# The first feed-forward's out product in two column blocks, four of 22 row pairs of each by seven products

## The chip, the cores and the metric

The kernel runs on one core of one Trainium2 chip. A core has a matrix engine (TensorE, PE in the profile; its weight loads are PEld), a vector engine (VectorE, DVE), a scalar engine (ScalarE, ACT), GpSimd (POOL) and SyncE (SP), which here issues most DMAs. Each engine runs its own instructions in order; semaphores tie them together. Operands lie in SBUF, sums of products in PSUM. The metric is the device time of one execution in microseconds (us), the median of several runs; lower is better.

## The reference

The layer takes x (256 positions of 2048 channels) and 256 memory positions:

```python
x += 1/2 * SwiGLU_1(rms(x))        # h = silu(gate) * up, 5632 wide; then h @ w_out
h = rms(x); p = h @ w_mix_in       # conv value | conv gate | gMLP u | gMLP v
x += concat(rms(conv(p)), rms(gmlp(p))) @ w_mix_out
x += CrossAttn_4heads(rms(x), rms(mem))
x += 1/2 * SwiGLU_2(rms(x))
out = rms_norm(x)
```

All in float32. The change concerns `h @ w_out` of the first SwiGLU, a product of 256 x 5632 by 5632 x 2048, and what stands right behind it: the first products of `w_mix_in`.

## The kernel before

**Products.** Each operand is kept as two parts, a rounded high part and the rest (low part), and a product of float32 matrices is three products of parts: high by high, high by low, low by high. ScalarE makes the high part by a cast, VectorE the low part by a subtraction (`weights`, lines 115 and 116, for weights; `split`, lines 123 and 124, for the other operand). A weight tile is 128 rows (one k) by 1024 columns or two k by 512, 512 KB, loaded by SyncE's queue into one of the "raw" tiles and split into an "hl" tile. TensorE uses it in twelve products of 128x128 by 128x512: two halves of the 256 positions, two halves of the columns (or two k), three products of parts.

**First feed-forward, in product.** The class `FeedForward` makes eleven column groups h0 to h10 of the hidden layer. Each h tile has 512 columns, that is four k of the out product. Within a group the 16 k go in eight pairs, some of them "S": a pair by `seven`, the others "C": by `eight`. A pair of k and a pair of column halves of 512 with the two halves of positions is a 2x2 by 2x2 block product, eight products; `seven` (Winograd's form of Strassen's scheme) makes it with seven, from sums of weight blocks (made on VectorE, lines 422 to 435) and from four sums of blocks of the other operand, "forms" or sides, that are made once. Its seven results gather in seven accumulators, "1" to "7", which are joined at the end with those of `eight` ("2", "3", "4", "8").

**Turns.** The out product needs h with its columns on the partitions. `turning` (line 293) makes four 128x128 transposes on TensorE into one PSUM tile "aux"; of these there are two. `split` then writes the result into hA, hB or hC: a cast on ScalarE, a subtraction on VectorE. A turn covers two k, so there are 22. Four are done in the last group of the in product.

**Out product.** `gemm_n` goes over four blocks of 512 columns, each over the 44 k two at a time (22 weight tiles): lines 190 to 192. In the first block one of the remaining 18 turns is issued after each weight tile (`between=turns`). Each block's result is copied by ScalarE into a tile o, turned in two turns, and joined to xT (`joins`, line 637) in the course of the next product:

```python
for n in range(4):
    acc = gemm_n(a["ffn1_w_out"][n], ff.of, per=0.8 if n else 0.0, between=turns, after=0 if n == 0 else 4)
    ...
    turns += [turning(o, 2 * i * P, joins(4 * n + 2 * i)) for i in range(2)]
```

Then the mix stage starts: `gemm_n` over the column groups of `w_mix_vg`, four products that also carry the last turns. `later`, `put` and `beside` hold a list of small jobs (squares of the memory rows, convolution taps) that are dealt out behind weight tiles by a cost in us.

**What sets the order.** The program is written as straight code for a tile framework; pools hand out buffers (wraw 4 weight tiles, whl 3 split tiles, ps 6 and pa 2 PSUM banks), and a scheduler lays out each engine's instructions from it.

Of the kernel before, what the change touches and what calls it, by code (L numbers as in the profile page):

```python
# [11 lines left out]
F32 = mybir.dt.float32  # L12
# [5 lines left out]
P = 128  # L18
# [20 lines left out]
SUMMED = ((2, 7, 13), (2, 7, 13))  # L39

# [29 lines left out]
def layer(ctx: ExitStack, tc: tile.TileContext, a: dict):  # L70
# [108 lines left out]
    def gemm_n(w, x_hl, per=0.0, between=None, after=4):  # L179

        acc = [ps.tile([P, 2, 256], F32, name="acc").rearrange("p a b -> p (a b)") for _ in range(2)]
        nk = w.shape[1]
        for k0 in range(0, nk, 2):
# [9 lines left out]
            if between and k0 >= after:  # L193
                between.pop(0)()
            beside(per)
        return acc
# [132 lines left out]
    class FeedForward:  # L329
# [6 lines left out]
        def __init__(self, stack, tags, x_hl, gain, w_in, pattern, summed):  # L336
# [41 lines left out]
        def raw(self, j, k):  # L378
            i = self.raw_at % (4 + len(self.raws))
            self.raw_at += 1  # L380
            raw = wraw.tile([P, 1024], F32, name="raw") if i < 4 else self.raws[i - 4]
            nc.sync.dma_start(out=raw, in_=self.w_in[j, :, k])
            return raw
# [28 lines left out]
        def x(self, k, t):  # L412
            s = slice(t * P, (t + 1) * P)
            return self.x_hl[:, k, 0, s], self.x_hl[:, k, 1, s]

        def seven(self, j, p, b, first, last):
# [8 lines left out]
            form = [(self.forms[self.spairs.index(p)][:, f, 0], self.forms[self.spairs.index(p)][:, f, 1]) for f in range(4)]  # L425
            three(b["5"], form[0], w[:, 0, lo], w[:, 1, lo], first, last)
            three(b["7"], form[2], w[:, 0, hi], w[:, 1, hi], first, last)
            nc.vector.tensor_tensor(out=one[:, lo], in0=sums[:, lo], in1=two[:, hi], op=ALU.add)
            w = self.parts(one)
            three(b["6"], form[1], w[:, 0, lo], w[:, 1, lo], first, last)  # L430
            three(b["1"], self.x(k, 0), w[:, 0, hi], w[:, 1, hi], first, last)
            w = self.parts(two)
            three(b["2"], self.x(k + 1, 0), w[:, 0, lo], w[:, 1, lo], first, False)
            three(b["3"], form[3], w[:, 0, hi], w[:, 1, hi], first, False)
            nc.vector.tensor_tensor(out=two[:, lo], in0=two[:, lo], in1=one[:, lo], op=ALU.subtract)
            w = self.parts(two, G)
            three(b["4"], self.x(k + 1, 1), w[:, 0, lo], w[:, 1, lo], first, False)
            if self.next is not None:
                with tc.issue_after(self.cast.ins):
                    self.summed(self.next)  # L440
                self.next = None

        def eight(self, j, p, b, first, last, plain):
            for k in (2 * p, 2 * p + 1):
                at = (j, k) in self.sums_at and self.sums_at.index((j, k))
                w = self.parts(self.raw(j, k), last=plain) if at is False else self.hls[at % len(self.hls)]
                begin = [(1, 1)] if first and k % 2 == 0 else []
                acc = [[b["2"], b["3"]], [b["4"], b["8"]]]
                by_two(acc, self.x_hl[:, k], w[:, 0], w[:, 1], k, begin, last and k % 2 == 1)
# [13 lines left out]

        def group(self, j, r, after=()):
            b = {}
            for name in "57":
                b[name] = bank(ps if name == "5" else pa, "acc" if name == "5" else "aux")
            b["6"] = bank(pa, "aux")
            for name in "1234":
                b[name] = bank(ps, "acc")  # L470
            b["8"] = bank(ps, "acc")
# [3 lines left out]
            for p, c in enumerate(self.pattern):  # L475
                if c == "S":
                    self.seven(j, p, b, p == 0, p == self.spairs[-1])
                    if p == self.spairs[-1]:
                        nc.scalar.copy(out=p1, in_=b["1"])
                        nc.vector.tensor_tensor(out=u2, in0=p1, in1=b["6"], op=ALU.add)  # L480
                        nc.vector.tensor_tensor(out=u4, in0=u2, in1=b["5"], op=ALU.add)
                        nc.vector.tensor_tensor(out=u2, in0=u2, in1=b["7"], op=ALU.add)
                        nc.vector.tensor_tensor(out=u5, in0=u2, in1=b["5"], op=ALU.add)
                else:
                    late = p > self.spairs[-1] and len(after) > 0
                    self.eight(j, p, b, p == self.pattern.index("C"), p == n - 1, late)
# [6 lines left out]
            self.give(j, (p1, u2), (u4, u5), r)  # L493

# [57 lines left out]
        def turn(self, i):  # L552

            def go():
# [10 lines left out]
                def both(tp):  # L565
                    tile, at = self.where(2 * i)
                    d = tile[:, at:at + 2]
                    split(d[:, :, 0], d[:, :, 1], tp)

# [14 lines left out]
    with ExitStack() as stack:  # L584
        ff = FeedForward(stack, ("S1", "S0", "S2"), x_hl, lambda k: gains[:, k:k + 1], a["ffn1_w_in"], PATTERNS[0], SUMMED[0])
# [45 lines left out]
        x_hl = gained_tile("S2")  # L631
        ss = st.tile([P, T], F32, name="ss", bufs=2)

        def joins(f):

            def go(tp):
# [3 lines left out]
                for k in range(f, f + 2):  # L640
                    gained(x_hl, k, xT[:, k], col("mix_norm", k))
# [3 lines left out]
        for n in range(4):  # L645
            acc = gemm_n(a["ffn1_w_out"][n], ff.of, per=0.8 if n else 0.0, between=turns, after=0 if n == 0 else 4)
            if n == 0:
                pool = stack.enter_context(ff.late)
                pool = stack.enter_context(tc.tile_pool(name="ffn1", bufs=1, reuse_waits="tile"))
            o = pool.tile([P, 2, G], F32, name="o", bufs=2)  # L650
            for t in range(2):
                nc.scalar.copy(out=o[:, t], in_=acc[t])
            turns += [turning(o, 2 * i * P, joins(4 * n + 2 * i)) for i in range(2)]
        ff.high.close()
# [4 lines left out]
    with ExitStack() as stack:  # L659
        with tc.tile_pool(name="mix", bufs=1) as pool:  # L660
# [70 lines left out]
            for n in range(NCT // 2):  # L731
                load_gate(n)
                later.appendleft((1.6, memory_parts(n)))
                acc = gemm_n(a["w_mix_vg"][n], lambda k: x_hl[:, k], per=1.35, between=turns, after=2)
# [423 lines left out]
def _laid_out(v):  # L1158
# [17 lines left out]
    a["ffn1_w_out"] = _tiled(g["ffn1_w_out"][0], 512)  # L1176
# [31 lines left out]
```

## Time and profile before

| | |
|---|---|
| median of 3 runs | 2100.37 us (2097.94 to 2103.01) |
| profiled execution, own time | 2096.62 us |
| its span | 2094.9 us |
| TensorE busy | 2082.5 us (99%) |
| VectorE busy | 1577.4 us (75%) |
| ScalarE busy | 1165.2 us (56%) |
| GpSimd busy | 67.7 us (3%) |
| moved by DMA | 442.34 MB |

The span runs from the first to the last instruction; the own time of the same execution is 1.7 us longer. Busy time of an engine that others wait for sets the time; busy time of the others matters only where they are late. The out product of the first feed-forward runs from 467 to 716 us of the span.

### The profile page before, as it was taken

Reading aid. Unit: us, or ns where it says so; the run is one execution under the profiler, and the core shown is the slowest. Engines: PE = TensorE matmul, PEld = TensorE weight load, DVE = VectorE, ACT = ScalarE, POOL = GpSimd, SP = SyncE. Lnnn points to the kernel's source line nnn. Section 1 sums busy time; section 2 is a strip of 40 time slices with the busy share of each in tenths; the row PEclk is TensorE's granted clock in tenths of the full one; section 3 lists DMA queues with packets and bytes.
Section 4 is the critical chain, followed back from the end, with each engine's and each line's share of the span. In section 5 each row is a group of like instructions: output and inputs, shape, how many; then the busy total and the mean of one; then the engine's idle time right before and its main releaser. Section 6 shows DMA issues by size and latency. Waiting matters only on the chain.

```text
span 2094.9 us, 26646 instructions
## 1 busy us (share of the span) xinstructions
PE 2082.5 (99%) x9786; PEld 1741.6 (83%) x9786; DVE 1577.4 (75%) x2217; ACT 1165.2 (56%) x1451; POOL 67.7 (3%) x83
## 2 busy tenths in 40 slices
PE   9999999999999999999999999999999999999998
PEld 7888888888888888888888898888888888888886
DVE  7888888875655589888877666778888888787754
ACT  8665666554544454445665454556665666554443
POOL 0000000000000000000000000000000000000000
PEclk9999999999999999999999999999999999999999
DMA  9787778755665666555555543576777777556664
GB/s 368 241 263 246 226 228 263 228 183 169 226 189 188 216 233 198 187 180 183 182 197 188 186 157 117 200 272 218 217 248 251 241 225 246 182 163 203 195 192 152
DMA packets 122387, 442.34 MB, mean 211 GB/s; under 512 B 13584, under 2 KB 13968, under 8 KB 121872
## 3 DMA queue, kind: packets, MB, share of 16 engines
q1 hardware_dynamic: 113040, 407.08, 57.0%
q0 software_dynamic: 8640, 32.51, 8.3%
q8 instruction: 76, 1.25, 0.2%
q10 hardware_dynamic: 576, 1.06, 0.1%
q14 instruction: 55, 0.45, 0.1%
HBM read 438.49 MB, written 2.10 MB: 210 GB/s over the span
## 4 chain that ended last, share of the span: by engine, by line
PE 96%; DMA 2%; issue 1%; ACT 1%; DVE 0%; POOL 0%; SPq 0%; DVEq 0%; ACTq 0%; POOLq 0%
PE acc L192 12%; PE acc L191 12%; PE acc L190 12%; PE acc L319 9%; PE acc L321 9%; PE acc L318 9%; PE acc L144 8%; PE acc L151 4%; PE acc L307 3%; PE acc L305 3%; PE acc L306 3%; PE aux L293 1%; PE aux L307 1%; PE aux L305 1%; PE aux L306 1%
## 5 line engine op out<-in xcount | busy, mean ns | idle before, releaser
L116 DVE TENSOR_TENSOR hl<-raw,hl 128x1024 fp32r<-128x1024 f32 (+1 forms) x402 | 488.5, 1216 | 277.3 <-ACT hl L115 276.3
L115 ACT CAST hl<-raw 128x1024 fp32r<-128x1024 f32 (+1 forms) x402 | 419.6, 1045 | 477.8 <-PE acc L192 291.0
L373 DVE TENSOR_TENSOR hl<-spare,hl 128x1024 fp32r<-128x1024 f32 (+1 forms) x128 | 146.6, 1149 | 34.0 <-ACT hl L372 31.0
L372 ACT CAST hl<-spare 128x1024 fp32r<-128x1024 f32 (+1 forms) x128 | 126.2, 994 | 69.4 <-PE acc L321 25.9
L319 PE MATMUL acc<-hl,x_hl 128*128 128x512 f32 x408 | 147.7, 391 | 0.3 <-DVE hl L124 0.2
L373 DVE TENSOR_TENSOR hl<-raw,hl 128x1024 fp32r<-128x1024 f32 (+1 forms) x107 | 120.7, 1131 | 29.7 <-ACT hl L372 28.3
L372 ACT CAST hl<-raw 128x1024 fp32r<-128x1024 f32 (+1 forms) x107 | 103.5, 979 | 69.6 <-PE acc L321 26.7
L318 PE MATMUL acc<-hl,x_hl 128*128 128x512 f32 x408 | 141.8, 390 | 0.3 <-ACT hl L123 0.3
L321 PE MATMUL acc<-hl,x_hl 128*128 128x512 f32 x408 | 126.5, 389 | 0.0
L372 ACT CAST ring<-spare 128x1024 fp32r<-128x1024 f32 (+1 forms) x81 | 80.4, 997 | 58.9 <-PE acc L321 19.0
L373 DVE TENSOR_TENSOR ring<-spare,ring 128x1024 fp32r<-128x1024 f32 (+1 forms) x81 | 93.0, 1153 | 13.9 <-ACT ring L372 12.6
L191 PE MATMUL acc<-hl,m_hl 128*128 128x512 f32 x256 | 100.3, 392 | 0.0
L191 PE MATMUL acc<-hl,x_hl 128*128 128x512 f32 x256 | 100.3, 392 | 0.0
L192 PE MATMUL acc<-hl,m_hl 128*128 128x512 f32 x256 | 100.2, 391 | 0.0
L192 PE MATMUL acc<-hl,x_hl 128*128 128x512 f32 x256 | 99.8, 390 | 0.0
L319 PE MATMUL acc<-ring,x_hl 128*128 128x512 f32 x248 | 91.4, 389 | 0.0
L190 PE MATMUL acc<-hl,m_hl 128*128 128x512 f32 x256 | 91.2, 392 | 0.0
L318 PEld LDWEIGHTS acc<-hl,x_hl 128*128 128x128 f32 x408 | 76.4, 188 | 16.6 <-ACT hl L123 0.5
L319 PEld LDWEIGHTS acc<-hl,x_hl 128*128 128x128 f32 x408 | 76.2, 188 | 16.8 <-DVE hl L373 0.8
L190 PE MATMUL acc<-hl,x_hl 128*128 128x512 f32 x256 | 90.0, 391 | 0.0
L321 PEld LDWEIGHTS acc<-hl,x_hl 128*128 128x128 f32 x408 | 76.6, 188 | 16.0
L318 PE MATMUL acc<-ring,x_hl 128*128 128x512 f32 x248 | 88.8, 389 | 0.0
(362 smaller groups left out, 4974.9 us busy)
## 6 DMA issues: line engine op xcount, KB each, us to landing
spare<-in_ffn_w_in SPq DMA_DIRECT2D x195, 512.0 KB, 7.0
raw<-in_ffn_w_out SPq DMA_DIRECT2D x176, 512.0 KB, 3.5
raw<-in_ffn_w_in SPq DMA_DIRECT2D x156, 512.0 KB, 6.4
hl_s<-in_ffn_w_in POOLq DMA_DIRECT2D x44, 512.0 KB, 8.8
raw<-in_w_mix_vg SPq DMA_DIRECT2D x32, 512.0 KB, 4.5
raw<-in_w_k SPq DMA_DIRECT2D x32, 512.0 KB, 3.6
raw<-in_w_v SPq DMA_DIRECT2D x32, 512.0 KB, 4.3
raw<-in_w_mix_out SPq DMA_DIRECT2D x32, 512.0 KB, 4.6
```

What stands on the lines that cost most here:

```text
L115: nc.scalar.copy(out=hl[:, 0, :size], in_=raw[:, :size])
L116: newest[0] = nc.vector.tensor_tensor(out=hl[:, 1, :size], in0=raw[:, :size], in1=hl[:, 0, :size].bitcast(F32), op=ALU.subtract)
L144: nc.tensor.matmul(acc, lhsT=hi[:, k], rhs=xs[k], start=first and k == 0, stop=last and k == kk - 1, skip_group_check=True,)
L151: nc.tensor.matmul(acc[:, 0], lhsT=lo[:, k], rhs=xs[k][:, 0], start=False, stop=last and k == kk - 1, skip_group_check=True,)
L190: nc.tensor.matmul(acc[t], lhsT=x[:, 0, s], rhs=hi[:, k], start=k0 + k == 0, stop=False)
L191: nc.tensor.matmul(acc[t], lhsT=x[:, 0, s], rhs=lo[:, k], start=False, stop=False)
L192: nc.tensor.matmul(acc[t], lhsT=x[:, 1, s], rhs=hi[:, k], start=False, stop=k0 + k == nk - 1)
L318: nc.tensor.matmul(acc[t][g], lhsT=x[:, 0, s], rhs=hi[:, cols[g]], start=(t, g) in first, stop=False)
L319: nc.tensor.matmul(acc[t][g], lhsT=x[:, 0, s], rhs=lo[:, cols[g]], start=False, stop=False)
L321: nc.tensor.matmul(acc[t][g], lhsT=x[:, 1, s], rhs=hi[:, cols[g]], start=False, stop=last)
L372: self.cast = nc.scalar.copy(out=hl[:, 0, :n], in_=raw[:, :n])
L373: newest[0] = nc.vector.tensor_tensor(out=hl[:, 1, :n], in0=raw[:, :n], in1=hl[:, 0, :n].bitcast(F32), op=ALU.subtract)
```

## The change

The out product is made in two blocks of 1024 columns. Each block goes over 22 pairs of k; pairs 9, 12, 15 and 18 are made by `seven`, the others by `eight`, with the eight accumulators of the in product ("6" and "7" in the two aux banks). The first block takes the pairs in order; the second starts with pair 9 and has the three others behind every second plain pair. The weights are laid out anew in memory for it. The sides of the four pairs are made when their k are turned (`out_sides`): a copy on ScalarE, four operations of 128x128 on VectorE, and two splits of 256 elements each. The remaining 18 turns are issued within the first seven pairs: three in each of the first four, two in each of the next three; behind pair 6 a pool is opened over memory of h4 to h10, for the sums of weights, two more raw tiles (raw_out) and the result. Three tiles of "more_out" take the place of x_hl meanwhile: two for split weights, the rest for the sides. The second block's result is joined in four turns during the first products of the mix stage; the first two of these are made in halves, first k 0 to 7 of both, then k 8 to 15.

In numbers of instructions: 24 products of 128x512 fewer on TensorE, 88 instructions more on VectorE, 22 more on ScalarE, the same number of DMAs. The orders of all engines are unchanged up to the start of the out product, and from the product by w_mix_out on.

```diff
+OUT_S = (9, 12, 15, 18)
+OUT_STEPS = (
+    list(range(KF // 2)),
+    [9, 0, 1, 12, 2, 3, 15, 4, 5, 18, 6, 7, 8, 10, 11, 13, 14, 16, 17, 19, 20, 21],
+)
...
-        def eight(self, j, p, b, first, last, plain):
+        def eight(self, j, p, b, last, plain, between=None):
             for k in (2 * p, 2 * p + 1):
+                if between is not None and k % 2 == 1:
+                    between()
...
+        def out_block(self, n, result, hook, between=None):
+            b = {}
+            self.begun = set()
+            steps = OUT_STEPS[n]
+            for i, p in enumerate(steps):
+                if p in OUT_S:
+                    if "5" not in b:
+                        self.banks(b, "57612348" if i == 0 else "5761")
+                    done = all(q not in OUT_S for q in steps[i + 1:])
+                    self.seven(NG + n, p, b, done)
+                    if done:
+                        o = result()
+                        places = [o[:, t, g * G:(g + 1) * G] for g in range(2) for t in range(2)]
+                        self.joins_sevens(b, *places)
+                else:
+                    if i == 0:
+                        self.banks(b, "2348")
+                    self.eight(NG + n, p, b, i == len(steps) - 1, False, between)
+                hook(i)
+            for acc, i in (("2", 0), ("3", 2), ("4", 1), ("8", 3)):
+                nc.vector.tensor_tensor(out=places[i], in0=places[i], in1=b[acc], op=ALU.add)
+            return o
+
+        def out_sides(self, form, tp):
+            f1, f2 = ev.tile([P, T], F32, name="tu"), ev.tile([P, T], F32, name="tg")
+            second = ev.tile([P, T], F32, name="sq")
+            nc.scalar.copy(out=second.rearrange("p (k t) -> p k t", k=2), in_=tp[:, :, P:])
+            a11, a21, a12, a22 = tp[:, 0, :P], second[:, :P], tp[:, 1, :P], second[:, P:]
+            f = [f1[:, :P], f1[:, P:], f2[:, :P], f2[:, P:]]
+            nc.vector.scalar_tensor_tensor(out=f[0], in0=a21, scalar=-1.0, in1=a22, op0=ALU.mult, op1=ALU.subtract)
+            nc.vector.scalar_tensor_tensor(out=f[1], in0=f[0], scalar=-1.0, in1=a11, op0=ALU.mult, op1=ALU.subtract)
+            nc.vector.tensor_tensor(out=f[2], in0=a11, in1=a21, op=ALU.subtract)
+            nc.vector.tensor_tensor(out=f[3], in0=a12, in1=f[1], op=ALU.subtract)
+            for i, both in enumerate((f1, f2)):
+                s = slice(2 * i, 2 * i + 2)
+                split(form[:, s, 0], form[:, s, 1], both.rearrange("p (f n) -> p f n", f=2))
...
-        for n in range(4):
-            acc = gemm_n(a["ffn1_w_out"][n], ff.of, per=0.8 if n else 0.0, between=turns, after=0 if n == 0 else 4)
...
+        def turns_first(i):
...
+            for _ in range(2 if i < 4 else 1):
+                next_turn()
+            if i == 6:
+                stack.enter_context(ff.late)
+                ff.high.close()
+                pool = rest["pool"] = stack.enter_context(tc.tile_pool(name="ffn1", bufs=1, reuse_waits="tile"))
+                ff.sums = pool.tile([P, 1024], F32, name="sums_out")
+                ff.raws += [pool.tile([P, 1024], F32, name=f"raw_out{q}") for q in range(2)]
...
+        o = ff.out_block(0, result, turns_first, next_turn)
+        turns += turned(o, 0)
...
+        o = ff.out_block(1, result, beside_second)
+        turns += turned(o, 1)
...
+            accs = []
+            for n in range(2):
+                load_gate(n)
+                later.appendleft((1.6, memory_parts(n)))
+                accs.append(gemm_n(
+                    a["w_mix_vg"][n], lambda k: x_hl[:, k], per=1.35, between=turns, after=0, ks=range(0, 8, 2), step=4
+                ))
```

**Turns in TensorE's order.** Before, in the first block of the out product, around the turns of h8 and h9 (h_128 and h_129 are their tiles, ident the identity matrix, hB the turned operand of this block's k):

```order
L192 MATMUL acc<-hl,hB 128x512
L190 MATMUL acc<-hl,hB 128x512 x2
L191 MATMUL acc<-hl,hB 128x512 x2
L293 MATMUL aux<-ident,h_128 128x128 x4
L293 MATMUL aux<-ident,h_129 128x128 x4
L192 MATMUL acc<-hl,hB 128x512 x2
L190 MATMUL acc<-hl,hB 128x512
L191 MATMUL acc<-hl,hB 128x512
L192 MATMUL acc<-hl,hB 128x512
```

Two turns stand together, and weight tiles of products ahead of and behind them. With the change, at the same point of the turns (first rows: the last products of k 13, last two rows: the first products of k 14):

```order
L329 MATMUL acc<-hl,hA 128x512 x2
L326 MATMUL acc<-hl,hA 128x512
L301 MATMUL aux<-ident,h_127 128x128 x4
L327 MATMUL acc<-hl,hA 128x512
L326 MATMUL acc<-hl,hA 128x512
L327 MATMUL acc<-hl,hA 128x512
L329 MATMUL acc<-hl,hA 128x512 x2
L301 MATMUL aux<-ident,h_128 128x128 x8
L301 MATMUL aux<-ident,h_129 128x128 x8
L301 MATMUL aux<-ident,h_130 128x128 x8
L326 MATMUL acc<-hl,hA 128x512 x4
L327 MATMUL acc<-hl,hA 128x512 x2
```

The six turns of h8, h9 and h10 have moved together, between the products of two weight tiles.

**Casts in ScalarE's order.** Before, for the turns of h7 to h10 (hB and hC from aux are the turns' casts, hl from raw those of weight tiles):

```order
L123 CAST hB<-aux 128x2x256 x2
L115 CAST hl<-raw 128x1024 x2
L123 CAST hB<-aux 128x2x256
L123 CAST hC<-aux 128x2x256
L115 CAST hl<-raw 128x1024 x2
L123 CAST hC<-aux 128x2x256 x2
L115 CAST hl<-raw 128x1024
L241 ACTIVATE sm<-raw 128x256
L244 ACTIVATE sq<-raw 128x256 x2
L115 CAST hl<-raw 128x1024
```

At most two casts of turns stand together there. With the change, from the copy for the sides of h7's second turn to the cast of the weight tile of k 14 (raw_out):

```order
L552 COPY sq<-aux 128x256
L131 CAST hB<-aux 128x2x256
L131 CAST more_out<-tu 128x2x128
L131 CAST more_out<-tg 128x2x128
L131 CAST hB<-aux 128x2x256
L131 CAST hC<-aux 128x2x256
L552 COPY sq<-aux 128x256
L131 CAST hC<-aux 128x2x256
L131 CAST more_out<-tu 128x2x128
L131 CAST more_out<-tg 128x2x128
L131 CAST hC<-aux 128x2x256 x2
L381 CAST hl<-raw_out_3907 128x1024
```

The cast of the weight tile has moved behind the casts of all six turns and of their sides (tu and tg).

**VectorE's order, with the change,** from the sides of h7's second turn to those of h9's first (before, VectorE had no such operations; the turns' subtractions stood between those of weight tiles):

```order
L555 SCALAR_TENSOR_TENSOR tu<-sq 128x128
L556 SCALAR_TENSOR_TENSOR tu<-tu,aux 128x128
L557 TENSOR_TENSOR tg<-aux,sq 128x128
L132 TENSOR_TENSOR hB<-aux,hB 128x2x256
L558 TENSOR_TENSOR tg<-aux,tu 128x128
L132 TENSOR_TENSOR more_out<-tu,more_out 128x2x128
L132 TENSOR_TENSOR more_out<-tg,more_out 128x2x128
L132 TENSOR_TENSOR hB<-aux,hB 128x2x256
L132 TENSOR_TENSOR hC<-aux,hC 128x2x256
L555 SCALAR_TENSOR_TENSOR tu<-sq 128x128
L556 SCALAR_TENSOR_TENSOR tu<-tu,aux 128x128
L557 TENSOR_TENSOR tg<-aux,sq 128x128
```

The last operation on the sides (line 558, which reads aux) has moved behind the subtraction of the turn that follows.

## Rows read from the trace of the kernel before

**Rows 1.** Page: span, and TensorE's busy time, share and instructions.

```profile
span 2094.9 us, 26646 instructions
...
PE 2082.5 (99%) x9786; PEld 1741.6 (83%) x9786; DVE 1577.4 (75%) x2217; ACT 1165.2 (56%) x1451; POOL 67.7 (3%) x83
```

**Rows 2.** Windows of the out product: us, PE, PEld, DVE, ACT, POOL busy, clock.

```profile
467.00:527.00 60.00, 60.00 (x301) 50.20 (x300) 37.18 (x43) 31.65 (x42) 0.00 (x0) 1.00 0.53 167
...
653.00:716.00 63.00, 63.00 (x285) 52.18 (x284) 33.08 (x40) 30.56 (x39) 0.00 (x0) 1.00 0.57 182
```

**Rows 3.** Waits of TensorE, the longest of six.

```profile
PE aux L219 <- DVE ones L216: 1.1, 1, 1.1
```

**Rows 4.** Timeline of TensorE in the out product's second block, weight tiles' starts.

```profile
563.40 0.62 PE L190 MATMUL acc<-hl,hB 128*128 128x512 f32 x2
...
579.72 0.62 PE L190 MATMUL acc<-hl,hB 128*128 128x512 f32 x2
```

**Rows 5.** Timeline of TensorE in the last group, a tile with a turn.

```profile
458.00 1.07 PE L318 MATMUL acc<-hl,x_hl 128*128 128x512 f32 x4
458.91 0.60 PE L293 MATMUL aux<-ident,h 128*128 128x128 f32 x4
...
461.20 0.62 PE L318 MATMUL acc<-hl,x_hl 128*128 128x512 f32 x2
```

**Rows 6.** Timeline of three engines, two turns in the out product.

```profile
508.50 1.03 PE L293 MATMUL aux<-ident,h 128*128 128x128 f32 x8
...
509.14 1.07 ACT L123 CAST hB<-aux 128x512 fp32r<-128x512 f32 x2 [0.29 <-PE aux L293]
...
510.02 1.28 DVE L124 TENSOR_TENSOR hB<-aux,hB 128x512 fp32r<-128x512 f32 x2
```

**Rows 7.** Groups by line and shape: busy, mean ns, idle before.

```profile
L116 DVE TENSOR_TENSOR hl<-raw,hl 128x1024 fp32r<-128x1024 f32 x396 | 484.5, 1224 | 270.1 <-ACT hl L115 269.0
L115 ACT CAST hl<-raw 128x1024 fp32r<-128x1024 f32 x396 | 416.0, 1052 | 470.3 <-PE acc L192 291.0 <-PE acc L144 38.8 <-ACT sq L244 24.2
...
L124 DVE TENSOR_TENSOR hB<-aux,hB 128x512 fp32r<-128x512 f32 x16 | 10.7, 685 | 0.2
...
L123 ACT CAST hB<-aux 128x512 fp32r<-128x512 f32 x16 | 9.1, 589 | 3.6 <-PE aux L293 3.6
...
L124 DVE TENSOR_TENSOR y_hl<-tg,y_hl 128x256 fp32r<-128x256 f32 x16 | 6.3, 416 | 0.0
...
L123 ACT CAST y_hl<-tg 128x256 fp32r<-128x256 f32 x16 | 6.1, 402 | 1.6 <-DVE tg L783 1.5
```

**Rows 8.** Instructions of lines 726 and 408: ns min/median/max.

```profile
L726 ACT COPY pad<-aux x8: 364/374/380, 749.4 to 814.9; 128x256 f32<-128x256 f32 x8
...
L408 DVE TENSOR_TENSOR spare<-spare x6: 282/284/287, 6.0 to 1384.7; 128x128 f32<-128x128 f32 x6
```

**Rows 9.** Window of the first feed-forward's in product.

```profile
8.00:441.00 433.00, 432.93 (x1909) 357.81 (x1908) 359.62 (x444) 276.69 (x319) 25.39 (x29) 1.00 0.79 253
```

**Rows 10.** Window of the mix stage's start; VectorE's timeline of a joined turn.

```profile
715.00:740.00 25.00, 25.00 (x118) 20.81 (x117) 15.02 (x23) 13.12 (x20) 0.93 (x7) 1.00 0.85 294
...
726.02 0.68 DVE L637 SCALAR_TENSOR_TENSOR xT<-aux,xT 128x512 f32<-128x512 f32 x1
726.62 0.48 DVE L269 SCALAR_TENSOR_TENSOR x_hl<-xT,pv,x_hl 128x256 fp32r<-128x256 f32 x1
727.01 0.42 DVE L245 TENSOR_TENSOR ss<-ss,sq 128x256 f32<-128x256 f32 x1
```

**Rows 11.** Weight DMAs of the out product, issue to landing.

```profile
DMA to landing us min/median/max: 3.2/3.5/6.2
```

**Rows 12.** Windows at the end; line 219, ns min/median/max.

```profile
2086.00:2088.00 2.00, 0.05 (x1) 0.00 (x0) 1.21 (x3) 1.97 (x4) 0.06 (x1) 1.00 0.31 129
...
2090.00:2092.00 2.00, 0.00 (x0) 0.00 (x0) 0.28 (x1) 0.00 (x0) 0.00 (x0) 0.50 0.87 322
...
L219 PE MATMUL aux<-ones x22: 274/421/583, 1.1 to 4.8; 128*128 128x128 f32 x22
```

More of the change, by code (lines that the diff above doesn't have):

```diff
@@ L192, in gemm_n @@
                     nc.tensor.matmul(acc[t], lhsT=x[:, 1, s], rhs=hi[:, k], start=False, stop=k0 + k == nk - 1)
-            if between and k0 >= after:
+            if between and k0 >= after and k0 % step == 0:
                 between.pop(0)()
@@ L381, in raw @@
             raw = wraw.tile([P, 1024], F32, name="raw") if i < 4 else self.raws[i - 4]
-            nc.sync.dma_start(out=raw, in_=self.w_in[j, :, k])
+            nc.sync.dma_start(out=raw, in_=self.w_in[j, :, k] if j < NG else self.w_out[j - NG, :, k])
             return raw
@@ L410, in sides, with x, half, begins @@
             split(self.forms[i][:, :, 0], self.forms[i][:, :, 1], f)
-        def x(self, k, t):
+        def x(self, j, k):
+            return self.x_hl[:, k] if j < NG else self.of(k)
+        def half(self, j, k, t):
             s = slice(t * P, (t + 1) * P)
-            return self.x_hl[:, k, 0, s], self.x_hl[:, k, 1, s]
-        def seven(self, j, p, b, first, last):
+            x = self.x(j, k)
+            return x[:, 0, s], x[:, 1, s]
+        def begins(self, name):
+            first = name not in self.begun
+            self.begun.add(name)
+            return first
+        def seven(self, j, p, b, last):
             k = 2 * p
@@ L640, in go @@
                 for k in range(f, f + 2):
-                    gained(x_hl, k, xT[:, k], col("mix_norm", k))
+                    gained(rest["x_hl"], k, xT[:, k], col("mix_norm", k))
                     square_into(ss, xT[:, k], k == 0)
             return go
-        for n in range(4):
-            acc = gemm_n(a["ffn1_w_out"][n], ff.of, per=0.8 if n else 0.0, between=turns, after=0 if n == 0 else 4)
[L647 to L653, printed above, removed]
@@ L654, in layer, with next_turn @@
-        ff.high.close()
+        ff.ring, ff.raws = [], []
+        def next_turn():
+            if turns:
+                turns.pop(0)()
+        def turns_first(i):
+            if i == 0:
+                more = big.tile([P, 4, 2, 1024], F32R, name="more_out", tag="S2")
+                ff.ring += [more[:, q] for q in range(2)]
+                forms = more[:, 2:].rearrange("p a two n -> p (a two n)")
+                ff.out_forms = [
+                    forms[:, q * 1024:(q + 1) * 1024].rearrange("p (f two n) -> p f two n", two=2, n=P) for q in range(4)
+                ]
+            for _ in range(2 if i < 4 else 1):
[6 more added lines that the diff above has]
+                ff.raws += [pool.tile([P, 1024], F32, name=f"raw_out{q}") for q in range(2)]
@@ new lines, in result, with turned, beside_second @@
+        def result():
+            return rest["pool"].tile([P, 2, 2 * G], F32, name="o", bufs=2)
+        def turned(o, n):
+            return [turning(o, 2 * i * P, joins(8 * n + 2 * i)) for i in range(4)]
+        o = ff.out_block(0, result, turns_first, next_turn)
+        turns += turned(o, 0)
+        def beside_second(i):
+            if i == OUT_STEPS[1].index(OUT_S[-1]):
+                ff.ring = []
+                rest["x_hl"] = gained_tile("S2")
+            elif i > 9:
+                beside(1.4)
+                if i % 2 == 0 and turns:
+                    turns.pop(0)()
```

78 lines of the change are left out of this document (45 added, 33 removed).

## Prediction

> **What bounds the kernel now.** I read the page first: of a span of 2094.9 us TensorE is busy 2082.5 [rows 1]. A stretch gets shorter only if TensorE has less to do in it, and longer if TensorE has to wait. Then the windows of the out product of the first feed-forward, the product that the change rewrites: in its first and in its last block TensorE is busy without a gap, with the granted clock at 1.00 (that is 2.4 GHz), while ScalarE and VectorE work about half of the time [rows 2]. Last the waits: the longest that TensorE has in the whole run is 1.1 us, at the start [rows 3]. So nothing can be gained there by hiding more; each product fewer gains its own time, as long as the new order adds no wait.
>
> **The gain: 24 products fewer.** The timeline of the out product shows the pace. Six weight tiles of twelve 128x512 products run from 563.40 to 579.72 [rows 4]: 16.32 / 72 = 0.2267 us each (the 0.39 printed beside one is its length in the pipeline, not its pace). A pair by seven products takes 21 where twelve and twelve stood; four pairs in each of two blocks save 8 x 3 = 24 products: 24 x 0.2267 = -5.4 us. Turns are moved, not removed: one costs TensorE what a tile with a turn takes above one without, 461.20 - 458.00 - 2.72 = 0.48 us [rows 5], and there are as many as before.
>
> **The seven-products' other work.** Each such pair adds sums of weights and a third and fourth split tile on VectorE and ScalarE. The in product of the same feed-forward is made in this way already, and from 8 to 441 TensorE is busy 432.93 of 433 us beside VectorE at 359.62 [rows 9], 83%. The new blocks mix one such pair with two or more plain ones, so their VectorE share is lower. I cost this at nothing; the cover is VectorE's free sixth. The weight DMAs are as many and as large as before, and land in 3.5 us, 6.2 at most [rows 11], against a ring of six buffers that each last 2.72 us: nothing.
>
> **The loss: six turns in a row.** This is the step on which I decide. Before, eighteen turns were spread over the first block, singly or in twos, with at least one weight tile of products behind each two. Now they are packed into seven pairs, and the last six (of h8, h9 and h10) stand in TensorE's order with no product between them: behind the weight tile of k 13, ahead of that of k 14 ("tile 14"). There are two "aux" tiles for them, so a turn can begin only when the one two before it has been read out: by ScalarE's cast, by VectorE's subtraction, and, for the four turns that make the sides of a seven (of these, the second of h7 just ahead and the first of h9), by three small operations more.
>
> The durations: two turns 1.03, so 0.5 each (0.45 of pace); ScalarE starts 0.64 after the first transpose; two casts take 1.07 and two subtractions 1.28 [rows 6], alone 0.59 and 0.68 [rows 7]. The cast of a 128x128 pair of sides is taken as that of y_hl, 0.40, its subtraction 0.42 [rows 7]; the copy of 256 elements is 0.37 and a small operation 0.28 [rows 8]. Let t = 0 be when TensorE reaches the first of the six.
>
> The second turn of h7 was made 3 us earlier. Its cast, copy, subtraction and first three small operations are through by -0.2, but its fourth, which frees its tile, stands in VectorE's order behind the subtraction of the turn at 0.
>
> Turn 1 of six: transposes 0 to 0.45, cast 0.64 to 1.23, subtraction to 1.93. The waiting small operation ends at 2.2: turn 2 starts at 2.2, turn 3 at 2.7.
>
> ScalarE casts turn 2 from 2.9 to 3.5, turn 3 to 4.1, and copies to 4.5. VectorE ends turn 2 at 4.2, so turn 4 starts there; VectorE goes on with turn 3 to 4.9 and its first three small operations to 5.8, subtracts turn 4 to 6.4, and makes the last small one to 6.7.
>
> Turn 5 starts at 6.7, turn 6 at 7.2. ScalarE casts them from 7.4 to 8.0 and to 8.5. Behind them in its order stands the cast of weight tile 14, 1.05 long [rows 7], which ends at 9.6. Only then do products go on. The low part of this tile ends 1.23 later [rows 7], at 10.8, where TensorE, having no more than four products by the high part, wants it at 10.5: 0.3 more.
>
> Of these 9.6 us TensorE's own work is 6 x 0.45 = 2.7, so the pause costs 9.6 - 2.7 + 0.3 = +7.2 us. Nothing else can fill it, since TensorE takes its instructions in order. Bounds: if sides never held a tile up, the circle of transposes, cast and subtraction is 1.9 us for two turns, the sixth turn would be at 4.3, tile 14's cast at about 6.7, and the pause 4.3; if the small operations that read PSUM take as long as the copy does, 0.37, and each hand-over costs a tenth more than I gave it, some 8.7. After the pause ScalarE and VectorE need 1.05 and 1.23 for a tile that lasts TensorE 2.72, so they get ahead again within two tiles, before the first seven (pair 9).
>
> In the first six pairs up to three turns go with two tiles. VectorE's load is then 2 x 1.23 + 3 x 0.64 + about 1.3 of sides = 5.7 us in 2 x 2.72 + 3 x 0.48 = 6.9. It fits: no wait.
>
> **The end of the product.** Four turns of the second block's result, not two, are joined while the mix stage begins. Before, VectorE was busy 15.02 of 25 us there; one joined turn costs it 0.68 and, for each of its two columns, about 0.4 and 0.35 by the starts: 2.2 [rows 10]. With two more turns and four additions of 0.64 it comes to 15.0 + 4.4 + 2.6 = 22 of 25. The first two products of the mix stage are halved, so that they need only columns that are joined already. It fits, with little to spare. I take nothing, and keep up to 3 us for the range.
>
> **Sum.** -5.4 + 7.2 = +1.8 us, from -1.1 to +3.3 by the bounds of the pause, to about +6 with the mix stage late. The profiled execution's own time is 2096.62 (its span and 1.7 around it): 2098.4. It is 3.75 under the median of the runs, 2100.37; on the median, 2102.2. What a measurement of this kernel can tell from no change is about 0.2%, 4.2 us: so most likely the same.
>
> **Rivals.** *The pause is hidden.* If the six turns were not to wait (ScalarE and VectorE so far ahead that buffers are free), the gain stands alone: 2100.37 - 5.4 = 2095.0, faster by 0.26%. For it: in the whole trace of before turns never made TensorE wait. Against it: they never came more than two at a time with products behind them, and two tiles cannot hold six turns. 0.05.
>
> *The clock falls in the pause.* TensorE is then mostly idle for some 9 us. The one place where it idles in this trace is the end: the clock is still 1.00 in the two microseconds after the last product and 0.50 (the 1.2 GHz level) in 2090 to 2092 [rows 12]. In the pause TensorE is never wholly at rest for more than about 2 us, which speaks against; that it is at work for less than a third of the time speaks for. What it would cost: at the kernel's start, out of rest, TensorE's small products last 583 ns at first and 274 at last, over some 4 us [rows 12]; products at half pace for as long lose about 2 us. 2102.2 + 2.0 = 2104.2, on the edge of slower. The Trainium skill ("TensorE: Matmul & The Clock Gate", section "HAM oscillation — how this bites in real kernels") says that waits between bursts of matmuls bring the clock down each time, and its Part 4 on PE-mode transpose that transposes don't count as work for the gate. By that rule this rival would be the forecast; no stretch of the trace of before has transposes alone, so it neither agrees nor differs. I give this rival 0.14.
>
> *VectorE falls behind at the mix stage's start, and the kernel is slower.* The 22 of 25 us worked out above are an average. Should the joins and the weight splits come 3 us late, TensorE waits at the halved products: 2102.2 + 3 = 2105.2, slower by 0.23%. It decides from a load of about 25.5 of 25 us on: 3.5 us more than I counted, say if the new additions and joins wait on each other. For it: VectorE was 60% busy there and is now to be near 90%. Against: ScalarE and VectorE get ahead of TensorE in the plain pairs before. 0.11.
>
> The pause alone, with nothing else: 0.70.
>
> **The chances.** Slower by over 0.2%: most of the third rival (0.09), half of the clock's (0.07), and the main case's upper end (0.03): 0.19. Faster: 0.05. Within: 0.76. The range reaches from the pause at its lower bound with a microsecond for the runs' scatter, 2098.2, to the third rival with as much, 2106.2.
>
> **What the changed profile would show.** TensorE's waits gain entries for "aux" on VectorE and ScalarE (tiles hB, hC and tg) and one for the cast and subtraction of a weight tile from raw_out, together 6 to 8 us, all between about 505 and 522 us; the four windows of the out product would read 60 of 60 but for that stretch; there are 24 products of 128x512 fewer, and the pace of the others is 0.2267. The granted clock of the stretch reads 1.00; if it reads less, the clock's rival is right. In the first 25 us of the mix stage TensorE has no gap; if it has, the third is right. The prediction is wrong if the turns wait less than 4 us in sum, or if waits stand at places that I cost at nothing: the sevens in the blocks, the border between the blocks (whose accumulators are drained there), the raw tiles.

## The result and the profile after

The changed kernel takes 2102.39 us (median of 22 runs, 2100.54 to 2104.83), the kernel before 2099.32 in the same sessions (22 runs). The ratio is 1.0014, 95% interval 1.0009 to 1.0020: slower by 3.1 us, within the 0.2% that I called the same. I had forecast 2102.2, that is 1.8 us more than before.

The page of the changed kernel answers to [rows 1]; TensorE's waits (us in total, times, longest) answer to [rows 3]:

```profile
span 2100.9 us, 26719 instructions
...
PE 2082.0 (99%) x9762; PEld 1740.4 (83%) x9762; DVE 1624.3 (77%) x2305; ACT 1179.5 (56%) x1473; POOL 67.7 (3%) x83
```

```profile
PE aux L301 <- DVE hB L132: 2.6, 2, 1.6
...
PE acc L326 <- ACT hl L381: 1.6, 1, 1.6
PE aux L301 <- DVE hC L132: 1.4, 1, 1.4
```

TensorE's work is 0.5 us less than before [rows 1], not 5.4, although it has 24 instructions fewer: products at a lower clock count as longer. And it waits 2.6 + 1.4 us for "aux" and 1.6 for a weight tile's cast, waits that the kernel before did not have.

The windows around them (us, busy time of PE, PEld, DVE, ACT, POOL, then the granted clock) stand against 60.00 of 60 at 1.00 in [rows 2]:

```profile
500.00:527.00 27.00, 21.36 (x97) 17.04 (x96) 18.89 (x35) 13.90 (x23) 0.00 (x0) 0.81 0.35 116
...
512.00:514.00 2.00, 0.69 (x6) 0.69 (x7) 1.82 (x7) 1.11 (x3) 0.00 (x0) 1.00 0.98 363
514.00:516.00 2.00, 1.03 (x7) 0.80 (x6) 1.64 (x3) 1.13 (x3) 0.00 (x0) 0.68 0.90 340
516.00:518.00 2.00, 0.60 (x4) 0.20 (x3) 1.62 (x6) 1.21 (x3) 0.00 (x0) 0.50 0.08 31
...
522.00:524.00 2.00, 2.00 (x6) 1.54 (x5) 2.00 (x3) 1.05 (x2) 0.00 (x0) 0.50 0.21 33
524.00:526.00 2.00, 2.00 (x8) 1.56 (x8) 2.00 (x3) 0.36 (x1) 0.00 (x0) 0.76 0.77 266
```

TensorE is busy 21.36 of 27 us. The clock is at its 2.4 GHz level until some point between 514 and 516, at the 1.2 GHz level (0.50) from 516 to 524, and back by 526. Before it fell, from 511 on, TensorE had made nothing but transposes, with waits between them. The timeline of that stretch shows each step of the pause (start, duration, engine, line; in brackets the idle time before it and what ended it):

```profile
509.46 0.60 PE L301 MATMUL aux<-ident,h 128*128 128x128 f32 x4
...
511.06 0.60 PE L301 MATMUL aux<-ident,h 128*128 128x128 f32 x4
...
512.57 0.68 DVE L132 TENSOR_TENSOR hB<-aux,hB 128x512 fp32r<-128x512 f32 x1
513.17 0.28 DVE L558 TENSOR_TENSOR tg<-aux,tu 128x128 f32<-128x128 f32 x1
513.31 1.09 PE L301 MATMUL aux<-ident,h 128*128 128x128 f32 x8 [1.65 <-DVE hB L132]
...
515.37 1.12 PE L301 MATMUL aux<-ident,h 128*128 128x128 f32 x4 [0.97 <-DVE hB L132]
...
517.14 0.69 DVE L132 TENSOR_TENSOR hC<-aux,hC 128x512 fp32r<-128x512 f32 x1
517.75 0.28 DVE L558 TENSOR_TENSOR tg<-aux,tu 128x128 f32<-128x128 f32 x1
517.88 1.97 PE L301 MATMUL aux<-ident,h 128*128 128x128 f32 x8 [1.40 <-DVE hC L132]
...
519.04 0.59 ACT L131 CAST hC<-aux 128x512 fp32r<-128x512 f32 x1 [0.57 <-PE aux L301]
...
519.89 0.59 ACT L131 CAST hC<-aux 128x512 fp32r<-128x512 f32 x1 [0.27 <-PE aux L301]
520.37 1.05 ACT L381 CAST hl<-raw_out 128x1024 fp32r<-128x1024 f32 x1
...
521.47 2.08 PE L326 MATMUL acc<-hl,hA 128*128 128x512 f32 x4 [1.62 <-ACT hl L381]
...
523.35 1.05 PE L327 MATMUL acc<-hl,hA 128*128 128x512 f32 x2
...
525.95 1.09 PE L326 MATMUL acc<-hl,hA 128*128 128x512 f32 x4
```

The second turn of h7 is at 509.46, the first of the six turns at 511.06. The fourth small operation of h7's sides (line 558) is behind a subtraction, as the order had it. The next two turns start at the end of that subtraction (513.25), which the trace names as what they waited for, and ahead of the small operation's end (513.45). It is the same with the last two turns: they start at 517.88, a subtraction ends at 517.83, line 558 at 518.03. The last two run at half pace: their transposes take 1.97 where two turns took 1.09 at 513.31. ScalarE's cast of k 14's weights (raw_out) starts right behind the last turn's cast, and products go on at 521.47, the first four in 1.88 us instead of 0.91. The products of k 15 begin at 525.95: 14.9 us for twelve products and six turns, which at full pace are 12 x 0.2267 + 6 x 0.45 = 5.4. The pause cost 9.5 us in this execution.

### The profile page after: what moved, and what is told of

It reads as the page before. It is cut to its first block, busy times and chain, and to the rows that moved or that the text cites. A ratio compares the mean times of both kernels' runs of the same rounds, so it can differ in the third digit from the quotient of the medians.

```text
span 2100.9 us, 26719 instructions
## 1 busy us (share of the span) xinstructions
PE 2082.0 (99%) x9762; PEld 1740.4 (83%) x9762; DVE 1624.3 (77%) x2305; ACT 1179.5 (56%) x1473; POOL 67.7 (3%) x83
## 4 chain that ended last, share of the span: by engine, by line
PE 83%; issue 13%; DMA 2%; POOL 1%; ACT 1%; DVE 1%; DVEq 0%; POOLq 0%; ACTq 0%
PE acc L327 10%; PE acc L326 10%; PE acc L329 10%; PE acc L199 8%; PE acc L200 8%; PE acc L198 8%; PE acc L152 8%; PE acc L159 4%; PE acc L314 3%; PE acc L315 3%; PE acc L313 3%; PE aux L301 1%; PE aux L315 1%; PE aux L314 1%; PE aux L313 1%
## 5 line engine op out<-in xcount | busy, mean ns | idle before, releaser
L123 ACT CAST hl<-raw 128x1024 fp32r<-128x1024 f32 (+1 forms) x314 | 327.1, 1043 | 356.2 <-PE acc L200 192.4
L124 DVE TENSOR_TENSOR hl<-raw,hl 128x1024 fp32r<-128x1024 f32 (+1 forms) x314 | 380.7, 1214 | 165.7 <-ACT hl L123 164.3
L382 DVE TENSOR_TENSOR hl<-raw,hl 128x1024 fp32r<-128x1024 f32 (+1 forms) x156 | 178.9, 1149 | 54.1 <-ACT hl L381 52.8
L381 ACT CAST hl<-raw 128x1024 fp32r<-128x1024 f32 (+1 forms) x156 | 153.6, 994 | 114.3 <-PE acc L329 48.5
```

The source lines that it names most:

```text
L123: nc.scalar.copy(out=hl[:, 0, :size], in_=raw[:, :size])
L124: newest[0] = nc.vector.tensor_tensor(out=hl[:, 1, :size], in0=raw[:, :size], in1=hl[:, 0, :size].bitcast(F32), op=ALU.subtract)
L381: self.cast = nc.scalar.copy(out=hl[:, 0, :n], in_=raw[:, :n])
L382: newest[0] = nc.vector.tensor_tensor(out=hl[:, 1, :n], in0=raw[:, :n], in1=hl[:, 0, :n].bitcast(F32), op=ALU.subtract)
```

## The experiments

Each ratio is to the kernel before, run on the same chip beside it, with its 95% interval.

**No pause.** Half of the turns go to PSUM banks that the first block does not use yet, and raw_out is used only from pair 9 on:

```diff
-    def turning(o, c, sink):
+    def turning(o, c, sink, bank=None):
...
-            tp = pa.tile([P, 2, T], F32, name="aux")
+            tp = ps.tile([P, 2, T], F32, name="acc") if bank else pa.tile([P, 2, T], F32, name="aux")
...
-                turning(self.h[i // 2], i % 2 * 2 * P, both)()
+                turning(self.h[i // 2], i % 2 * 2 * P, both, i > 4 and i % 4 > 1)()
...
-                ff.raws += [pool.tile([P, 1024], F32, name=f"raw_out{q}") for q in range(2)]
+            if i == 8:
+                ff.raws += [rest["pool"].tile([P, 1024], F32, name=f"raw_out{q}") for q in range(2)]
```

> The changed kernel with the two spare PSUM banks used for half of the turns (four tiles instead of two), and raw_out in use only from pair 9 on. TensorE's order has no two turns side by side any more. Theory (24 products gained, all lost again in the pause before k 14): no wait over 0.5 us in the out product, clock 1.00 there, and the full gain, 2099.3 - 5.4 = 2093.9 us, ratio to before 0.9974. Rival (the sevens' sums and splits give back part of their gain elsewhere, so that the pause was not the whole loss): 2096 or more, with TensorE's waits in pairs 9 to 18, at the border of the blocks or at the mix stage's start.

Measured: 0.9972 [0.9961, 0.9983]. TensorE's row of the page, and the window that answers to the one above:

```profile
PE 2077.0 (99%) x9762; PEld 1738.0 (83%) x9762; DVE 1623.2 (78%) x2305; ACT 1176.4 (56%) x1473; POOL 67.7 (3%) x83
...
500.00:527.00 27.00, 27.00 (x131) 22.28 (x130) 19.16 (x30) 13.99 (x20) 0.00 (x0) 1.00 0.52 160
```

No gap, the clock at 1.00, and no wait of TensorE in the product or in the mix stage. The whole gain is there: TensorE's 2077.0 us are 5.5 below those of the kernel before [rows 1], and 0.28% of 2099.3 is 5.9 us (3.6 to 8.2 by the interval), where 5.4 were worked out. This version is faster than both kernels.

**Half of the sevens, without the pause.** The same, with

```diff
-OUT_S = (9, 12, 15, 18)
+OUT_S = (15, 18)
...
-    [9, 0, 1, 12, 2, 3, 15, 4, 5, 18, 6, 7, 8, 10, 11, 13, 14, 16, 17, 19, 20, 21],
+    [15, 0, 1, 12, 2, 3, 9, 4, 5, 18, 6, 7, 8, 10, 11, 13, 14, 16, 17, 19, 20, 21],
```

> The version without the pause (four tiles for the turns, raw_out from pair 9 on), with sevens at pairs 15 and 18 only: 12 products of 128x512 more. Theory (each product left out gains its pace and nothing else): 12 x 0.2267 = 2.7 us more than that version, ratio to before 0.9972 + 0.0013 = 0.9985. Rival (a seven's extra sums and splits eat a part of its gain): less than 1.5 us more.

Measured: 0.9984 [0.9975, 0.9993]. The difference of the two ratios, 0.0012, is 2.5 us for 12 products, 0.21 each; their pace was 0.2267. By the medians of the two sessions, each against its own kernel before, it is 1.9 us. The theory gives 2.7, the rival less than 1.5; the medians speak for the theory, but the intervals overlap, so the rival is not ruled out.

**raw_out later, alone.** Two aux tiles as in the change, raw_out from pair 9 on (only the last part of the first diff).

> The changed kernel with raw_out in use only from pair 9 on, two aux tiles as before; still three turns in each of the first pairs of the program. Theory (the six turns stand in a row since k 14's weights need the memory pool that is opened behind all turns): products of k 14 to 17 come between the turns again, and only three turns stay in a row, ahead of the first seven, whose sums need that pool. Pause there about 4 us, so 2099.3 - 5.4 + 4 = 2098 us, ratio 0.9994. Rival (three turns in each pair are what makes the row): the six turns still wait, 2102.4.

Measured: 1.0008 [0.9999, 1.0018]. The waits:

```profile
PE acc L313 <- ACT hl L381: 3.1, 1, 3.1
...
PE aux L301 <- DVE hC L132: 1.0, 1, 1.0
```

A row of the windows behind the longer wait (the clock is the third figure from the end), and of TensorE's timeline there the first and the last of fourteen products and the one that follows:

```profile
530.00:532.00 2.00, 2.00 (x6) 1.61 (x6) 2.00 (x3) 1.36 (x2) 0.00 (x0) 0.50 0.05 8
...
528.57 0.79 PE L313 MATMUL acc<-hl,more_out 128*128 128x512 f32 x1 [3.08 <-ACT hl L381]
...
534.38 0.45 PE L314 MATMUL aux<-hl,more_out 128*128 128x512 f32 x1
534.66 0.39 PE L315 MATMUL aux<-hl,more_out 128*128 128x512 f32 x1
```

The six turns no longer stand in a row; three do, before the first seven, and the waits there are 3.1 + 1.0 us, as expected. So the number of turns in a pair of the program did not make the row: what made it is that products further on needed a tile of the pool. The time, though, failed the expectation: it came out 3 us above 2098, and the interval leaves out 0.9994. The clock fell here too, which the expectation did not count: the fourteen products from 528.57 to 534.66 take 6.1 us, where their pace gives 3.2. The gain of 5.4, the waits of 4.1 and these 2.9 us add up to +1.6 us, a ratio of 1.0008.

**Four tiles for the turns, alone** (the first two parts of the first diff).

> The changed kernel with four tiles for the turns and nothing else (raw_out used from k 14 on, as in the change). Theory (both the two tiles and raw_out's place behind all turns make the pause): turns no longer stand in a row, but k 14's cast still waits behind the last two turns' casts: TensorE waits about 2 us there, 2099.3 - 5.4 + 2 = 2096 us, ratio 0.9984. Rival (the two tiles alone are the cause): no wait, ratio 0.9972.

Measured: 1.0008 [0.9999, 1.0017]. Neither came true. The turns no longer wait, but TensorE waits as long for something else, 5.2 us. ScalarE's cast of k 14's tile, of this run:

```profile
513.36 7.32 SPq L392 DMA_DIRECT2D raw_out<-in_ffn_w_out  x3
...
518.03 1.04 ACT L381 CAST hl<-raw_out 128x1024 fp32r<-128x1024 f32 x1 [3.18 <-DMA raw_out<-in_ffn_w_out]
```

It waited 3.18 us for the DMA. SyncE issued this DMA at 513.36, in its order behind others, 0.4 us after VectorE had split k 13 (511.73 to 512.96) and a raw tile had come free; it landed near 518. In the change the same split ended at 510.42, the DMA was issued at 510.83, and the turns hid it. (That it was the raw tile which held SyncE up is read from these times, and wasn't tried by itself.) Two late things lay on top of each other, and taking away one showed the other.

In this wait the clock fell as well, with no row of transposes ahead of it:

```profile
516.00:518.00 2.00, 0.00 (x0) 0.00 (x0) 0.00 (x0) 0.00 (x0) 0.00 (x0) 1.00 1.02 420
518.00:520.00 2.00, 0.88 (x2) 0.79 (x3) 0.90 (x1) 1.97 (x2) 0.00 (x0) 0.68 0.21 84
520.00:522.00 2.00, 2.00 (x6) 1.51 (x6) 2.00 (x4) 1.00 (x2) 0.00 (x0) 0.50 0.35 53
```

K 14's twelve products, from 519.12 to 523.36, take 4.2 us instead of 2.7. The gain of 5.4, the wait of 5.2 and these 1.5 add up to +1.3 us, a ratio of 1.0006.

**No sides in the row.** The change with sevens at pairs 9 and 12 only (OUT_S = (9, 12)): the six turns make no sides.

> The changed kernel with sevens at pairs 9 and 12 only: 12 products more, and no sides among the six turns in a row (those of pairs 15 and 18 are gone). Theory (sides hold the aux tiles and ScalarE's and VectorE's orders): the time from the first of the six turns to k 14's first product falls from 10.4 to 7 us, and 12 x 0.2267 = 2.7 us of products come back: 2102.4 - 3 + 2.7 = 2102 us. Rival (the circle of two aux tiles alone sets the pause): pause unchanged, 2105.

Measured: 1.0011 [1.0002, 1.0020]. Of TensorE's timeline:

```profile
511.11 1.06 PE L301 MATMUL aux<-ident,h 128*128 128x128 f32 x8
...
515.17 1.71 PE L301 MATMUL aux<-ident,h 128*128 128x128 f32 x8 [0.81 <-DVE hC L132]
518.50 2.07 PE L326 MATMUL acc<-hl,hA 128*128 128x512 f32 x4 [1.62 <-ACT hl L381]
```

From the first of the six turns to k 14's products it is 7.4 us, not 10.4: the sides' part of the pause is as I had it, 3 us, and the time moved by -0.0003 (-0.6 us; expected -0.4). The rival's 2105, a ratio of 1.0027, lies outside the interval.

**Work in the pause, to keep the clock.** Four products that nobody uses follow the cast of each of the six turns:

```diff
+        def fill(turn):
...
+            x = ff.of(2 * turn)
+            rest["wide"] = ff.hA[:, 0].rearrange("p two t -> p (two t)")
+            for q in range(4):
+                nc.tensor.matmul(rest["idle"], lhsT=x[:, 0, :P], rhs=rest["wide"], start=True, stop=True)
...
```

> The changed kernel with four products that nobody uses (128x512, into a spare PSUM bank) behind the cast of each of the six turns, so that TensorE has work in the pause; all else the same. Theory (the clock's fall in the pause costs about 2 us on top of the waits): granted clock 1.00 from 510 to 530, products behind the pause at 0.2267 us, 2102.4 - 2 = 2100.4 us, ratio to before 1.0005. Rival (the clock's record falls, but costs nothing beside the waits): 2102.4, or more by the added products.

Measured: 1.0074 [1.0060, 1.0087], by the ratios some 14 us slower than expected, and much of it far from the edit: the first turn of the last group, long before, was already 5.4 us late. Products that read hl_s took 396 ns instead of 389; a new tile of 4 bytes had moved hl_s and others by 32 bytes. So the same with that tile padded:

> The run with unused products in the pause once more, with its one new small tile padded to 64 bytes, so that no other tile's address moves against 64 (before, 32 bytes of shift came with products of 396 ns instead of 389 wherever hl_s was read). Theory (clock costs about 2 us on top of the waits): granted clock 1.00 from 510 to 530, ratio to before 1.0014 - 0.0009 = 1.0005, and the time from the first of the six turns to the end of k 14's products about 1.2 to 2 us shorter than in the change. Rival (the shift of addresses was not what made that run slow): 1.007 again.

Measured: 1.0070 [1.0057, 1.0084]. The expectation failed: padding to 64 bytes did not bring the pace back. In both runs the clock stayed at 1.00, though, and the stretch from the first of the six turns to k 15's products was 13.7 us long instead of 14.9, with products in the pause that the change does not have. Then without any new tile:

> The run with unused products in the pause, its one new read written into a small tile that exists already, so that no tile's address moves at all. Theory (the clock costs about 2 us on top of the waits; the slowness of the two earlier runs of this kind came from moved addresses): granted clock 1.00 from 510 to 530, ratio to before 1.0005, and k 14's products at full pace. Rival (the added products themselves make the kernel slow): 1.007 again.

Measured: 1.0015 [1.0006, 1.0023]. So the added products are not what made the two others slow. But the gain is not there either. Windows and timeline of this run:

```profile
516.00:518.00 2.00, 1.68 (x12) 1.33 (x11) 1.48 (x5) 1.15 (x4) 0.00 (x0) 1.00 0.00 0
518.00:520.00 2.00, 2.00 (x13) 1.56 (x12) 2.00 (x6) 1.13 (x3) 0.00 (x0) 1.00 0.00 0
520.00:522.00 2.00, 1.03 (x5) 0.49 (x3) 0.79 (x3) 0.74 (x2) 0.00 (x0) 1.00 0.00 0
...
518.54 0.60 PE L301 MATMUL aux<-ident,h 128*128 128x128 f32 x4
519.17 0.59 ACT L131 CAST hC<-aux 128x512 fp32r<-128x512 f32 x1 [0.63 <-PE aux L301]
...
521.26 0.20 ACT L593 ACTIVATE warm<-ones 128x1 f32<-128x1 f32 x1 [1.50 <-DVE warm L748]
...
522.45 1.20 PE L326 MATMUL acc<-hl,hA 128*128 128x512 f32 x4 [1.42 <-ACT hl L381]
...
525.67 1.08 PE L326 MATMUL acc<-hl,hA 128*128 128x512 f32 x4
```

The clock stays at 1.00 through the pause, and k 14's products, from 522.45 to 525.67, take 3.2 us instead of 4.5 (521.47 to 525.95). But the read into the old tile "warm" made another instruction of ScalarE, which stands ahead of k 14's cast, wait 1.50 us for VectorE. That eats what the clock gave. The price of the clock's fall can be put together from these traces. The change's 4.5 us for k 14's products are 1.3 more than here, and 1.0 more than in the padded run, where they take 3.5. In the last turns ScalarE's cast starts 0.63 us after the transposes do (518.54 to 519.17), in the change 1.16 (517.88 to 519.04); two turns at half pace so put the last cast about 0.9 later. Together that is about 2 us, an estimate. The 1.2 us by which the whole stretch was shorter in the two runs before are less; the unused products stood in it there. That the price would come off the time is not shown.

**Addresses.** An unused tile in the kernel before, and no other edit:

```diff
     st.tile([P, 8], F32, name="to_64")
+    st.tile([P, 16], F32, name="pad")
```

> The kernel before with an unused tile of 64 bytes a partition, which moves the tiles hl_s, hC and more from multiples of 512 bytes by 64. No instruction is added. Theory (addresses made the two runs with unused products slow): products that read these tiles take about 396 ns instead of 389, and the whole is some 8 to 10 us slower, ratio 1.004 to 1.005. Rival (addresses don't matter): 1.000.

Measured: 1.0065 [1.0051, 1.0079]. With 32 elements, 128 bytes:

> The same with an unused tile of 128 bytes. It tells which multiple matters: at 1.000 the tiles have to lie on multiples of 128 bytes; at the ratio of the 64-byte run, on more.

Measured: 1.0056 [1.0044, 1.0069]. From 30 to 440 us TensorE is busy throughout in all three kernels, but gets through fewer products (x of the second column; the first row is the kernel before, the second the one with 64 bytes):

```profile
30.00:440.00 410.00, 409.93 (x1808) 338.82 (x1807) 341.27 (x412) 255.55 (x285) 25.39 (x29) 1.00 0.78 246
```

```profile
30.00:440.00 410.00, 410.00 (x1788) 335.47 (x1787) 336.89 (x407) 254.35 (x282) 25.39 (x29) 1.00 0.78 243
```

By line, products that read hl_s show a median of 392 to 396 ns with 64 bytes, where the kernel before shows 389; those that read hA or hB, whose addresses did not move, show 389 in both. So addresses alone make a kernel as slow as the two slow runs were. Which multiple the tiles need stays open: 128 bytes is not enough, and a shift by a full 512 was not tried.

**The mix stage's halves undone**, in the version without the pause: the first product of the mix stage whole, with the four turns behind its first weight tiles.

> The version without the pause, with the first two products of the mix stage whole again (all of k 0 to 15 of the first, with the four turns behind its first four weight tiles). Theory (the end of the product costs nothing, in halves or not, as the average load of VectorE there is under 25 of 25 us): ratio to before as without this edit, 0.9972, waits of TensorE from 710 to 740 under 0.5 us. Rival (the halves cover a wait of about 3 us for the joined columns): 0.9986, with TensorE waiting for x_hl there.

Measured: 0.9972 [0.9961, 0.9982], the same as with halves. The one wait of TensorE there, at 740.3, is 0.5 us for a weight tile's subtraction:

```profile
PE acc L199 <- DVE hl L124: 0.5, 1, 0.5
```

VectorE had room enough. The halves bring nothing here that can be measured.

## Why the prediction came out as it did

**The gain, -5.4 us: right.** Without the pause TensorE's work is 5.5 us less and the ratio 0.9972, that is -5.9, and half of the sevens bring about half of it. The sevens' other work costs nothing that the runs show. Neither do the raw tiles once they are used from pair 9 on, the border between the blocks, and the mix stage, where VectorE was to be busy 22 of 25 us. It was 21.97, with no wait of TensorE (changed kernel; the mix stage starts at 721.6):

```profile
721.00:746.00 25.00, 25.00 (x120) 20.65 (x119) 21.97 (x37) 16.38 (x29) 0.93 (x7) 1.00 0.76 236
```

**The pause: right in place, and in size but for the clock; in mechanism with one link wrong.** By the steps of the working, counted from the first of the six turns: the second was forecast at 2.2 and came at 2.25; the fourth at 4.2, came at 4.3; the fifth at 6.7, came at 6.8. The last cast of a turn was to end at 8.5 and ended at 9.4, k 14's cast at 9.6 and ended at 10.4. The slip is in the last two turns: from the start of their transposes to ScalarE's cast it is 1.16 us, where I took 0.64, because their transposes ran at half the pace. I had 7.2 us for the whole, and 9.5 were lost in the profiled execution; the 2.3 between them are about what the clock's fall costs.

The wrong link: I had a turn wait for the one two before it, and so the second and the fifth of the six for the last small operation on the sides (line 558). By the trace they waited for the subtraction of the turn just before them, and started while line 558 was not yet done. In VectorE's order the two stand side by side, so the times differ by 0.2 us at most, and the steps came out; that much is luck. The sides do hold the turns up, as the run without them shows by its 3 us, but through their place in the two engines' orders and, as far as the waits show it, the tile that they keep meanwhile. One reading was wrong as well: I had h7's second turn 3 us ahead of the first of the six; it is 1.6 (509.46 to 511.06), the turn and the five products that the order shows. Its third small operation ended 1.6 us after the first of the six began, not 0.2 before.

TensorE's waits add up to 5.6 us, not 6 to 8. The turns' own part is 4.0, right at the limit under which I had called the prediction wrong; the rest of the 9.5 is transposes and products that ran longer than at full pace.

**The clock: the step that failed.** The main case had it at 1.00, and I gave its fall 0.14, because TensorE was never to rest longer than about 2 us. It did not (its longest wait there was 1.65), and the clock fell all the same: all of the 22 runs show a mean clock of 0.996 to 0.998, where the profiled execution of before shows 0.999. So the rival that I called "the clock falls in the pause" is what happened, on top of the main case. From 511.06 on TensorE had only transposes and the clock fell to 0.50, while in the runs with unused products between them it stayed at 1.00. The Trainium skill ("TensorE: Matmul & The Clock Gate", Part 4 on PE-mode transpose) says that transposes don't count as TensorE being busy in the same way; the trace fits that, but doesn't show it. No run here tells transposes from too little work of any kind, and with four tiles for the turns the clock fell in a plain wait. My price for the fall was 2.0, and about 2 is what the traces give.

**The sum** is forecast +1.8, measured +3.1 (1.9 to 4.2 by the interval). With the clock's fall at its price it would have been +3.8; the profiled execution's pause gives -5.4 + 9.5 = +4.1. Both lie inside the interval. That the forecast of 2102.2 lies so near to 2102.39 is luck: it leaves out the clock, and its base was 1.05 too high, as over more runs the kernel before is 2099.32, not 2100.37.

**What I did not see.** I had the landing of k 14's tile as no limit. It was none in the change; with the turns out of the way it is the next wait, nearly as long.

## What to carry to other kernels

A gain on the engine that bounds a kernel is real, but it shows only where the new order adds no wait: read in the order of each engine what stands in a row with nothing between, and count how many buffers that row has. Where products need a tile of a pool that opens behind other work, that work was here pulled into one place ahead of them, however it was spread in the program; what helped was to use such a tile later and to have more buffers, both together. When one wait is removed, ask what would have been late at the same place, here a DMA. And count the clock into every pause: in three of these versions it cost some 1.5 to 2.9 us on top of the wait, worked out from their traces.

## What the runs showed of the hardware that I had not expected

The clock falls in a stretch of transposes with waits of up to 1.65 us between them, without any longer rest; in another version it falls in one wait of 4.9 us. In the changed kernel products resume at 521.47 at half pace, and the clock is at 1.00 again from 526 on. And an unused tile of 64 or 128 bytes a partition, which moves hl_s, hC and more (among others) off multiples of 512 bytes, makes the whole kernel 0.65% and 0.56% slower (13.6 and 11.7 us): with 64 bytes, products that read hl_s show a median of 392 to 396 ns instead of 389, and the pace of all products from 30 to 440 us falls by 1.1% (1788 instead of 1808).
